# The second query-key product on 64 rows, in a two-group attention block

## The chip, the core and the metric

The kernel runs on one core of one Trainium2 chip. The metric is the time on the device in microseconds (us). A second number is the span of a profiled execution, from its first to its last instruction.

Five engines work side by side: TensorE (PE in the profile, with its weight loads shown apart as PEld), VectorE (DVE), ScalarE (ACT), GpSimd (POOL), and SyncE (SP), which only issues transfers here. A matmul on PE takes a stationary tile, loaded ahead of it by a weight load, and a moving tile; the dimension that is summed over lies on the partitions, of which there are 128. A "row" below is one such partition.

## The reference

One layer of a hybrid encoder block on 1024 tokens of width 1024: one input projection, two kinds of attention of 8 heads each, gates, an output projection, and a layer norm. Cut to what matters:

```python
h = einsum('bsd,de->bse', x, w_in)
q_a, k_a, v_a, z_a, q_b, k_b, v_b, z_b = split(h)
# group A: tokens form a 16 x 64 grid, each query sees a window of 8 x 16
s = einsum('bqhd,biqjhd->bhqij', q_r, k_win) * scale + rel_bias
y_a = softmax(s) @ v_win
# group B: |i - j| <= 128, rotary q and k, 2 key heads for 8 query heads, a sink logit
s = einsum('bnqkgd,bnjkd->bnkgqj', qb, k_band) * scale, masked
y_b = softmax([s, sink])[..., :-1] @ v_band
mixed = concatenate([y_a * silu(z_a), y_b * silu(z_b)])
x = layer_norm(alpha * x + mixed @ w_out)
```

All is float32, and a head has 64 dimensions. To keep that precision on faster products, the kernel splits each operand into a high part in float16 (or a rounded float32) and a low part, the rest after the high part is taken off.

## The kernel before

**Stages.** First comes the value projection, in rounded float32. Then 21 column groups of the input projection (`ORDER`) are computed by `project`, each for two halves of the tokens: 48 products per group, three per chunk of the contraction (high by high, high by low, low by high; L354). Six groups run before the attention stage, and the other fifteen run within it as filler between attention products. The output projection (L889) and the layer norm end the kernel.

**The attention stage** is a loop over 128 units (`unit_list`): 64 of the windowed group "b", then 64 of the neighbourhood group "a". A unit is 128 queries of one head. Step i of the loop (L1023) issues the query-key products of unit i (`stage_qk`), the split and transpose of the probabilities of the unit before it (`stage_tr`), for every fourth step the probability-value products of four earlier units (`stage_pv`, L767), as many projection products as a table allows (`pump_to`), and the exponential of unit i (`stage_exp`).

**The stacked tiles.** Pair p holds two heads, j = 0 and 1, which come out of the projection on partitions 0 to 63 and 64 to 127. For each head the kernel keeps three float16 tiles of 128 partitions. In the code a names the 64 partitions on which the head is made (64j to 64j + 63), and o the other 64.

- `qs` (`split_q`): the high part of q on a, the low part on o.
- `ks` "kh" (`split_k`): the high part of k on a, and a copy of it on o.
- `ks` "kl" (`split_k`): the low part of k on a, and a copy of it on o.

Two products of 128 rows, accumulated in one bank of PSUM, then give (high q + low q) by high k (L704) and (high q + low q) by low k (L705). Both use the same 128 queries of `qs` as the stationary tile; the moving tile is 256, 384 or 288 columns of "kh" or "kl". DVE's fused bias, scale and row minimum (L712) reads the sum.

**Who makes them.** For the neighbourhood group, `split_k` is called with no rotary step (`dep` is None): ACT writes the high part out of PSUM (L233), DVE the low part (L239), and POOL copies each to the other 64 partitions (`dup_`, L271). For the windowed group the source is the rotated k; ACT makes the high part (L235), DVE or POOL the low one (L241), and POOL copies both. The windowed k is made once, in the first six groups, for its two heads and two halves of tokens, and each of its heads serves four heads of q, two with j = 0 and two with j = 1; the neighbourhood k of four pairs, two heads and two halves within the attention stage.

**Order.** The order of instructions on each engine is the order in which the program issues them. Within the loop, small operations wait in a list per engine (`enq`) and `pop` issues a few per step: two on POOL, one or two on DVE and ACT. An operation can be popped once those that it depends on were issued in an earlier step. `need` issues an operation, and what it depends on, at once where a later stage can't go on without it: before the first unit of a head, `need(*stk_ops[...])` (L1047 to L1050) forces out whatever of the stacked tiles isn't issued. A bank for the projection is reused once the operations that read it (`groups`) are issued; for k these are the low-part operations.

Of the kernel before, what the change touches and what calls it, by code (L numbers as in the profile page):

```python
# [53 lines left out]
def hybrid_block(ctx, tc, xT, x, wt, wv, wo, bias, sink, gain, lbias, cos, sin, bmask, out):  # L54
    nc = tc.nc
# [10 lines left out]
    def bank(tag):  # L66
        bufs = {"pj": 2, "s": 4, "t": 2}[tag]
        return (ps1 if bufs == 1 else ps2).tile([128, 512], F32, tag=tag, name=f"ps_{tag}", bufs=bufs)
# [68 lines left out]
    def enq(eng, fn, *deps, prio=1, after=0):  # L137
        op = Op(eng, fn, deps, prio)
        if clock["step"] is not None:
            queues[eng].append(op)  # L140
        elif after:
            events.setdefault(ran[0] + after, []).append(op.emit)
        else:
            op.emit()
        return op
# [10 lines left out]
    def need(*ops):  # L156
        for op in ops:
            if op.step is None:
                need(*op.deps)
                queues[op.eng].remove(op)  # L160
                op.emit()
# [35 lines left out]
    w_ops, stk_ops, load_ops = {}, {}, {}  # L197
# [27 lines left out]
    def own(kind, p, j):  # L225
        if (kind, p, j) not in stks:
            stks[kind, p, j] = stk(kind)
        return stks[kind, p, j]

    def split_hl(h, l, src, scaled, eng):  # L230
        def hi():
            if scaled:
                nc.scalar.activation(h(), src, AF.Copy, scale=QSCALE)  # L233
            else:
                nc.scalar.copy(h(), src)  # L235

        def lo():
            if scaled:
                nc.vector.scalar_tensor_tensor(l(), src, QSCALE, h(), op0=ALU.mult, op1=ALU.subtract)  # L239
            else:  # L240
                (nc.gpsimd if eng == "pool" else nc.vector).tensor_sub(l(), src, h())  # L241

        return hi, lo
# [15 lines left out]
    def split_k(p, half, src, dep=None):  # L259
        sl = slice(512 * half, 512 * half + 512)  # L260
        ops = []
        prio = 0 if dep is None else 1
        eng = "pool" if dep and clock["step"] is not None else "dve"
        for j in range(2):
            a, o = slice(64 * j, 64 * j + 64), slice(64 - 64 * j, 128 - 64 * j)
            hi, lo = split_hl(lambda j=j, a=a: own("kh", p, j)[a, sl], lambda j=j, a=a: own("kl", p, j)[a, sl],
                              src[a], dep is None, eng)

            def dup_(w, j=j, a=a, o=o):
                t = own(w, p, j)  # L270
                nc.gpsimd.tensor_copy(t[o, sl], t[a, sl])  # L271

            o1 = enq("act", hi, dep, prio=prio, after=28 if dep else 0)
            o2 = enq(eng, lo, o1, prio=prio, after=32 if dep else 0)
            ops.append(o2)
            dup = [enq("pool", lambda d=dup_: d("kh"), o1, after=32 if dep else 0),
                   enq("pool", lambda d=dup_: d("kl"), o2, after=36 if dep else 0)]
            stk_ops.setdefault((p, j, half), []).extend(dup)
        return ops

    def rope(ps, half):
# [12 lines left out]
    def evac(name, half, ps):  # L294
        sl = slice(512 * half, 512 * half + 512)
        kind = name.rstrip("0123")
        p = int(name[-1]) if name[-1].isdigit() else 0
        n = ORDER.index(name)
        if kind in ("kb", "qb"):
            raw, o1, o5 = rope(ps, half)  # L300
            if kind == "kb":
                split_k("b", half, raw, o5)
            else:
                split_q(f"b{p}", half, raw, o5)
            return [o1]
        if kind == "k":
            return split_k(p, half, ps)
        if kind == "q":
            return split_q(p, half, ps)
        e = 4 + p if kind == "zb" else p  # L310
        if half == 0:
            zt[e] = zslot(f"z{e}", ZTAG.get(name, "z"))
        if name in ORDER[:3]:
            nc.scalar.activation(zt[e][:, sl], ps, AF.Silu, scale=inv[:, n:n + 1])
            return []
        half_inv = invt[:, 0:1] if n < NPRO else invt[:, 1:2]
        o = enq("act", lambda: nc.scalar.activation(zt[e][:, sl], ps, AF.Tanh, scale=half_inv), prio=0)
        o2 = enq("dve", lambda: nc.vector.scalar_tensor_tensor(
            zt[e][:, sl], zt[e][:, sl], 1.0, ps, op0=ALU.add, op1=ALU.mult), o, prio=0)
        stk_ops.setdefault(name, []).append(o2)  # L320
        return [o2]
# [58 lines left out]
    with ExitStack() as vctx:  # L380
# [5 lines left out]
        ps = bank("t")  # L386
# [139 lines left out]
        for i in range(8):  # L526
# [5 lines left out]
            ps = bank(tags[i])  # L532
# [124 lines left out]
    def geom(u):  # L657
        g, p, j, t, _ = u
        if g == "a":
            b, half = t  # L660
            w = WINW[b]
            return NKEY[b], [4 * w] * 3
        lo, hi = max(t - 1, 0), min(t + 2, 8)
        return 128 * (hi - lo), [128] * (hi - lo)
# [19 lines left out]
    def stage_qk(u):  # L684
        g, p, j, t, _ = u
        n, _c = geom(u)
        ps = bank("s")
        if g == "a":
            b, half = t
            q = stks["q", p, j][:, 512 * half + 128 * b:512 * half + 128 * b + 128]  # L690
            sl = [stks[w, p, j].rearrange("p (r c) -> p r c", c=GW)[
                :, 4 * half:4 * half + 12, WIN0[b]:WIN0[b] + WINW[b]] for w in ("kh", "kl")]
            bias_t, op = st.pop((u, "b"))
            need(op)
            init = 3e38
        else:
            q = stks["q", f"b{p}", j][:, 128 * t:128 * t + 128]
            lo = max(t - 1, 0) * 128
            kv = p // 2
            sl = [stks[w, "b", kv][:, lo:lo + n] for w in ("kh", "kl")]  # L700
            bias_t = bm[:, 128 if t == 0 else 0:(128 if t == 0 else 0) + n]
            h = 2 * p + j
            init = nsk[:, h:h + 1]
        nc.tensor.matmul(ps[:, :n], q, sl[0], start=True, stop=False)  # L704
        nc.tensor.matmul(ps[:, :n], q, sl[1], start=False, stop=True)  # L705
        s0 = sns[units.index(u) % 2]
        sn = s0[:, 384 - n:]
        if g == "b" and t < 2:
            nc.vector.tensor_copy(s0[:, 384:385], nsk[:, h:h + 1])
        nm = ap.tile([128, 1], F32, tag="nm", name="nm", bufs=6)  # L710
        c = min(p, 1) if g == "b" else 2
        nc.vector.tensor_tensor_reduce(sn[:, :n], ps[:, :n], bias_t, sg[:, c:c + 1], init,  # L712
                                       op0=ALU.add, op1=ALU.min, accum_out=nm)
        st[u, "sn"] = sn
        st[u, "ps"] = ps
        st[u, "nm"] = nm
# [28 lines left out]
    def quad(q):  # L745
        g, p, j, t, _ = units[4 * q]
        return g, p, j, t // 4 if g == "b" else t[0] // 2
# [275 lines left out]
    for i in range(-LD, NU + LO):  # L1023
# [21 lines left out]
        if i < NU:  # L1045
            u = units[i]
            if u[3] in (0, 4):  # L1047
                need(*stk_ops[f"b{u[1]}", u[2], u[3] // 4])
            if u[3] == (0, 0):
                need(*stk_ops[u[1], u[2], 0], *stk_ops[u[1], u[2], 1])  # L1050
            stage_qk(u)
        q, m = divmod(i - LP - 3, 4)
# [9 lines left out]
        if m in (0, 2) and 0 <= q < NU // 4:  # L1062
            g, p, j, h = quad(q)
# [88 lines left out]
```

## Time and profile before

| what | value |
|---|---|
| median of three runs | 466.0 us (464.41 to 466.36) |
| the profiled execution | 467.47 us |
| its span | 465.7 us |
| mean granted clock of TensorE | 0.992 |
| matmuls on PE | 3239 |
| L704 and L705, executions each | 128 |
| copies of L271 on POOL | 40, between 107.7 and 332.2 us |
| first and last second product (L705) | 124.7 and 365.8 us |

In a row of grouped instructions stand the line, the engine, the operation, the tiles written and read, the shape and the count; then the busy time, the mean of one in ns, and the idle time of the engine just ahead of them with what ended it. "128*128 128x384" means a stationary tile of 128 rows by 128 columns and a moving tile of 128 rows by 384 columns. PE's records overlap: one starts before the one ahead has ended, so the distance between two starts, and not the length of a record, is what a product takes of the engine's time. A line of the table by stretches gives the stretch, its length, and for each engine the busy time and number of instructions, then the granted clock.

### The profile page before, as it was taken

How to read it: one execution, taken by the hardware profiler on the slowest of the kernel's cores; microseconds unless marked ns; L12 is line 12 of the kernel's file. 1: busy time of each engine (PE TensorE's matmuls, PEld its weight loads, DVE VectorE, ACT ScalarE, POOL GpSimd, SP SyncE). 2: the span in 40 equal slices, each digit the busy share in tenths (PEclk: the TensorE clock that was granted, in tenths of full speed). 3: DMA queues.
4: the chain of work that ended last, by engine and by line, in shares of the span. 5: the costliest groups of instructions: out<-in, count | busy, mean ns of one | idle time of the engine just before them, and what ended most of it. 6: DMA issues, size and time to landing. Idle time of an engine off the chain costs nothing.

```text
span 465.7 us, 9385 instructions
## 1 busy us (share of the span) xinstructions
PE 447.5 (96%) x3239; PEld 294.5 (63%) x3239; DVE 336.8 (72%) x807; ACT 288.3 (62%) x665; POOL 228.4 (49%) x235
## 2 busy tenths in 40 slices
PE   8999999999999899999999999999998789999992
PEld 6999964444455555555655555555465578888882
DVE  4887947439987677787888878877778349099734
ACT  4748569766588767887778777776877424012101
POOL 0004934638668459685246676445835244007621
PEclk9999999999999999999999999999999899999998
DMA  7887287971178999454799899999999995004511
GB/s 232 285 308 277 82 269 252 302 249 29 62 135 223 232 219 156 85 100 101 137 201 199 178 197 204 207 188 207 199 215 194 207 300 209 0 1 145 195 60 52
DMA packets 136463, 82.61 MB, mean 177 GB/s; under 512 B 101344, under 2 KB 117728, under 8 KB 136160
## 3 DMA queue, kind: packets, MB, share of 16 engines
q1 hardware_dynamic: 136272, 81.87, 74.0%
q8 instruction: 25, 0.41, 0.4%
q14 instruction: 22, 0.18, 0.2%
q10 hardware_dynamic: 144, 0.15, 0.1%
HBM read 51.58 MB, written 9.96 MB: 132 GB/s over the span
## 4 chain that ended last, share of the span: by engine, by line
PE 86%; DMA 5%; DVE 4%; issue 2%; ACT 2%; SPq 0%; DVEq 0%; ACTq 0%
PE ps_pj L354 43%; PE ps_s L889 8%; PE ps_t L767 6%; PE ps_s L428 6%; PE ps_pj L889 5%; PE ps_t L889 5%; DMA tr<-split 4%; PE ps_s L704 4%; PE ps_s L705 4%; PE ps_pj L428 3%; PE ps_t L428 3%; PE ps_t L787 1%; DMA xraw<-in_xT 1%; DVE qs L239 1%; ACT split L738 1%
## 5 line engine op out<-in xcount | busy, mean ns | idle before, releaser
L354 PE MATMUL ps_pj<-xf,wh 128*128 128x512 f16 x672 | 202.1, 379 | 0.9 <-DVE qs L239 0.6
L354 PE MATMUL ps_pj<-xf,wl 128*128 128x512 f16 x336 | 127.3, 379 | 0.0
L354 PEld LDWEIGHTS <-wh 128*128 128x128 f16 x672 | 63.5, 98 | 62.1 <-DVE ks L239 1.0
L728 ACT ACTIVATE ps_s<-sn,nm 128x385 f32<-128x385 f32 (+3 forms) x128 | 70.3, 549 | 37.6 <-DVE nm L712 36.7
L739 DVE SCALAR_TENSOR_TENSOR split<-ps_s,split 128x384 f16<-128x384 f32 (+2 forms) x128 | 65.7, 513 | 30.7 <-ACT split L738 29.4
L738 ACT ACTIVATE split<-ps_s 128x384 f16<-128x384 f32 (+2 forms) x128 | 57.5, 449 | 5.6 <-DMA tr<-split 4.0
L354 PEld LDWEIGHTS <-wl 128*128 128x128 f16 x336 | 32.9, 98 | 37.5
L712 DVE CUSTOM_DVE_ANT_0 sn<-ps_s,bm,nsk 128x384 f32<-128x384 f32 (+1 forms) x64 | 40.8, 637 | 7.9 <-PE ps_s L705 7.4
L712 DVE CUSTOM_DVE_ANT_0 sn<-ps_s,bias,sg 128x288 f32<-128x288 f32 (+1 forms) x64 | 36.0, 563 | 13.8 <-PE ps_s L705 6.7
L767 PEld LDWEIGHTS <-tr 128*128 128x128 f16 (+1 forms) x1104 | 37.1, 98 | 10.7 <-DMA tr<-split 7.5
L889 PE MATMUL ps_s<-wo,m 128*128 128x512 f32 (+1 forms) x192 | 43.6, 379 | 0.0
L185 POOL TENSOR_SCALAR wr<-wr,wsc 128x512 f32<-128x512 f32 x26 | 20.6, 792 | 41.8 <-ACT wh L180 33.8
L704 PE MATMUL ps_s<-ks,qs 128*128 128x384 f16 (+2 forms) x128 | 40.0, 312 | 0.0
L705 PE MATMUL ps_s<-ks,qs 128*128 128x384 f16 (+2 forms) x128 | 39.9, 312 | 0.0
L889 PEld LDWEIGHTS ps_s<-wo,m 128*128 128x128 f32 x192 | 34.3, 188 | 6.9
L944 ACT ACTIVATE sd<-mv,eps 128x1 f32<-128x1 f32 x8 | 2.4, 295 | 52.0 <-DVE mv L942 48.0
L186 POOL TENSOR_TENSOR wl<-wr,wh 128x512 f16<-128x512 f32 x26 | 32.6, 1255 | 2.2
L679 POOL TENSOR_SCALAR bias<-bias,rsg 128x576 f32<-128x576 f32 (+1 forms) x24 | 19.2, 798 | 28.1 <-DMA bias<-in_bias 24.2
L271 POOL COPY ks<-ks 64x512 f16<-64x512 f16 x40 | 26.8, 673 | 10.6 <-DVE ks L239 4.3
L981 POOL TENSOR_TENSOR xr<-xr,gb 128x512 f32<-128x512 f32 x7 | 10.3, 1480 | 40.7 <-ACT xr L978 40.7
L889 PE MATMUL ps_pj<-wo,m 128*128 128x512 f32 (+1 forms) x120 | 30.2, 390 | 0.0
L428 PE MATMUL ps_s<-wvh,x 128*128 128x320 f32 x128 | 29.6, 310 | 0.0
(147 smaller groups left out, 831.1 us busy)
## 6 DMA issues: line engine op xcount, KB each, us to landing
xraw<-in_xT SPq DMA_DIRECT2D x31, 256.0 KB, 4.5
ws<-in_wt SPq DMA_DIRECT2D x15, 512.0 KB, 5.4
wr<-in_wt SPq DMA_DIRECT2D x26, 256.0 KB, 3.3
bias<-in_bias SPq DMA_DIRECT2D x16, 288.0 KB, 3.7
wor<-in_wo SPq DMA_DIRECT2D x16, 256.0 KB, 4.2
xr<-in_x SPq DMA_DIRECT2D x8, 512.0 KB, 5.2
out<-xr SPq DMA_DIRECT2D x14, 256.0 KB, 2.2
bias<-in_bias SPq DMA_DIRECT2D x8, 384.0 KB, 4.2
```

What stands on the lines that cost most here:

```text
L186: nc.gpsimd.tensor_sub(l, raw, h)
L271: nc.gpsimd.tensor_copy(t[o, sl], t[a, sl])
L354: nc.tensor.matmul(ps, a[:, k % 4, :], mv, start=(k == 0 and i == 0), stop=(k == KT - 1 and i == 2))
L428: nc.tensor.matmul(ps[:, :320], lh[t // 4, k][:, ts], rh[k][:, cs], start=(k == 0 and i == 0), stop=(k == KT - 1 and i == 2))
L704: nc.tensor.matmul(ps[:, :n], q, sl[0], start=True, stop=False)
L705: nc.tensor.matmul(ps[:, :n], q, sl[1], start=False, stop=True)
L712: nc.vector.tensor_tensor_reduce(sn[:, :n], ps[:, :n], bias_t, sg[:, c:c + 1], init, op0=ALU.add, op1=ALU.min, accum_out=nm)
L728: nc.scalar.activation(pt[:, :m], sn[:, :m], AF.Exp, bias=nm, scale=-1.0, accum_out=sm[:, k:k + 1])
L738: nc.scalar.activation(hl[:, :m, 0, :c], src, AF.Copy, scale=PSCALE)
L739: nc.vector.scalar_tensor_tensor(hl[:, :m, 1, :c], src, PSCALE, hl[:, :m, 0, :c], op0=ALU.mult, op1=ALU.subtract)
L767: nc.tensor.matmul(ps[:, HD * m:HD * m + HD], a, b_, start=(i == 0), stop=(i == len(mms) - 1))
L889: nc.tensor.matmul(ps, lh[:, ts], rh[:, cs], start=(e == EO[0] and i == 0), stop=(e == EO[-1] and i == 2))
```

## The change

The second product takes only the 64 rows a, on which the high part of q and the first copy of the low part of k lie; low q by low k is no longer computed. `stage_qk` slices both operands:

```diff
         nc.tensor.matmul(ps[:, :n], q, sl[0], start=True, stop=False)
-        nc.tensor.matmul(ps[:, :n], q, sl[1], start=False, stop=True)
+        lo = slice(64 * j, 64 * j + 64)
+        nc.tensor.matmul(ps[:, :n], q[lo], sl[1][lo], start=False, stop=True)
```

In `split_k` the copy of the low part is issued only with a rotary step, so for the windowed k; for the neighbourhood k, the operation that a unit needs is then the low part itself:

```diff
-            dup = [enq("pool", lambda d=dup_: d("kh"), o1, after=32 if dep else 0),
-                   enq("pool", lambda d=dup_: d("kl"), o2, after=36 if dep else 0)]
-            stk_ops.setdefault((p, j, half), []).extend(dup)
+            stk_ops.setdefault((p, j, half), []).append(enq("pool", lambda d=dup_: d("kh"), o1, after=32 if dep else 0))
+            if dep:
+                o2 = enq("pool", lambda d=dup_: d("kl"), o2, after=36)
+            stk_ops[p, j, half].append(o2)
```

The windowed k needs its second copy of the low part: a head of q has its high part on the partitions that its own j gives, and the head of k that it uses may have been made on the other 64. In the neighbourhood group q and k of a head share j. The number of products, their columns, and every transfer stay as they were.

## The prediction

> **What bounds the kernel now.** I read the page's first part, then a table of engine time by stage, and then one stretch of the attention stage in order of time. On the first two lines, TensorE (PE) is busy for 96% of the span, well ahead of VectorE (DVE).
>
> ```profile
> span 465.7 us, 9385 instructions
> PE 447.5 (96%) x3239; PEld 294.5 (63%) x3239; DVE 336.8 (72%) x807; ACT 288.3 (62%) x665; POOL 228.4 (49%) x235
> ```
>
> A share over the whole span hides where the engine is full, so the next view cuts the stage in which the changed product runs, 124 to 378 us, into three stretches. The columns are length, busy time of each engine with its instruction count, granted clock, DMA share and rate.
>
> ```profile
> core 0: us, PE busy (x) PEld busy (x) DVE busy (x) ACT busy (x) POOL busy (x), PEclk, DMA share, GB/s
> 124.00:174.00 50.00, 48.46 (x388) 26.75 (x387) 38.10 (x111) 39.33 (x98) 28.98 (x28) 1.00 0.86 191
> 174.00:354.00 180.00, 179.14 (x1635) 103.38 (x1633) 145.47 (x402) 141.40 (x366) 107.88 (x123) 1.00 0.93 171
> 354.00:378.00 24.00, 18.53 (x154) 13.27 (x152) 11.29 (x31) 10.11 (x27) 8.35 (x7) 0.93 1.16 215
> ```
>
> From 174 to 354 us PE is busy for 179.14 of 180 us at a granted clock of 1.00. Nothing added to PE here has idle time to fall into: it lengthens the kernel one for one. GpSimd (POOL) is busy for 107.88 of the same 180 us, and no share of the chain that ended last is its own:
>
> ```profile
> PE 86%; DMA 5%; DVE 4%; issue 2%; ACT 2%; SPq 0%; DVEq 0%; ACTq 0%
> ```
>
> A busy PE can still be slack if its records are padded, so the third view is PE alone, in order of time, at 338 to 347 us. Each line has start, duration, line, tiles, stationary rows*columns, moving shape.
>
> ```profile
> 338.15 0.29 PE L705 MATMUL ps_s<-ks,qs 128*128 128x288 f16 x1
> 338.28 1.22 PE L767 MATMUL ps_t<-va,tr 96*128 96x64 f16 x36
> 339.33 0.38 PE L354 MATMUL ps_pj<-xf,wl 128*128 128x512 f16 x1
> ...
> 340.41 0.33 PE L704 MATMUL ps_s<-ks,qs 128*128 128x384 f16 x1
> 340.57 0.33 PE L705 MATMUL ps_s<-ks,qs 128*128 128x384 f16 x1
> 340.74 0.38 PE L354 MATMUL ps_pj<-xf,wh 128*128 128x512 f16 x1
> 340.95 0.38 PE L354 MATMUL ps_pj<-xf,wl 128*128 128x512 f16 x1
> ...
> 345.60 1.22 PE L767 MATMUL ps_t<-va,tr 128*128 128x64 f16 x36
> 346.65 0.38 PE L354 MATMUL ps_pj<-xf,wl 128*128 128x512 f16 x1
> ```
>
> The second query-key product (L705) starts 0.16 us after the first (L704), and the projection product behind it 0.17 us later, while each record lasts 0.33 us. So each product is let into the array about 0.16 us before the one ahead of it has ended: 0.33 - 0.16 = 0.17 us of every record is a tail under the next product. This overlap is what the change may disturb.
>
> **The change, part by part.** *The second product at 64 rows.* All 128 executions of L705 drop from 128 contraction rows to 64: rows 0 to 63 of the stacked tiles for the first head of a pair, rows 64 to 127 for the second. The moving columns stay 256 to 384, so I look at what fewer rows do to the streaming itself:
>
> ```profile
> L705 PE MATMUL ps_s<-ks,qs 128*128 128x384 f16 x80 | 26.1, 326 | 0.0
> L705 PE MATMUL ps_s<-ks,qs 128*128 128x288 f16 x32 | 9.5, 296 | 0.0
> L705 PE MATMUL ps_s<-ks,qs 128*128 128x256 f16 x16 | 4.4, 273 | 0.0
> L767 PE MATMUL ps_t<-va,tr 96*128 96x64 f16 x288 | 11.6, 193 | 4.8 <-DMA tr<-split 2.8 <-DMA va<-vwin 2.0
> L767 PE MATMUL ps_t<-va,tr 128*128 128x64 f16 x288 | 11.2, 193 | 1.1 <-DMA tr<-split 1.1
> ```
>
> A probability-value product of 96 rows lasts 193 ns, and so does one of 128 rows. Fewer rows save no streaming: 128 x 0 = 0 us.
>
> *The switch from 128 rows to 64 and back.* No row of this trace shows a 64-row product, so I bound it. Lower end: zero. In the stretch above, a block of 36 products of 96 rows between products of 128 rows takes 339.33 - 338.28 = 1.05 us until the next product starts, and a block of 36 with 128 rows 346.65 - 345.60 = 1.05 us, so going to 96 rows and back costs nothing visible. Upper end: the overlap is lost at each switch, so the next product starts only when the one ahead has ended, and its weight load can't be pulled ahead either. The first is 0.17 us. For the second, a run of weight loads has the rate:
>
> ```profile
> 259.55 1.20 PEld L767 LDWEIGHTS <-tr 96*128 96x128 f16 x36
> ...
> L705 PEld LDWEIGHTS <-qs 128*128 128x128 f16 x128 | 12.6, 99 | 14.4
> ```
>
> That is 1.20 / 36 = 0.033 us each, where a record alone reads 0.099 us. So the upper end is 0.17 + 0.03 = 0.20 us a switch. With two switches a unit (into the 64-row product and out of it, since a projection, transpose, probability-value or first query-key product of more rows always follows) there are 2 x 128 = 256. The ends are 0 and 256 x 0.20 = 51 us.
>
> I take the middle, 0.10 us a switch, for this reason. 96 rows starting at partition 0 can be run as the whole array with a quarter left empty. A product whose rows start at partition 64, as for half of the units, enters half-way, and I count on the array being emptied of the 128-row product first. Of the 0.17 us tail, part is the way into the array, which the next product could still overlap, so I take about half of it with a part of the weight load: 256 x 0.10 = 25.6 us. Few of the switches fall into idle time: in the stretch 354 to 378, where PE has 24.00 - 18.53 = 5.5 us idle, the second product runs only six times:
>
> ```profile
> 354.00:378.00 24.00, 2.20 (x6) 0.70 (x6) 0.93 1.16 215
> ```
>
> That hides at most 12 x 0.10 = 1.2 us; I count half, 0.6 us. Sum for the switches: 25 us.
>
> The page "TensorEngine Tiling (Array Packing)" of the Trainium skill, under Key Properties, says that changing the tiling mode drains TensorE, and lists 128, 64 and 32 rows as modes; 96 is not among them, which would explain the free block above. The page "TensorE: Matmul & The Clock Gate" of the Trainium skill, under Phases on the wall clock, gives the drain as about 128 cycles, at 2.4 GHz 53 ns; an estimate by that page alone would be 256 x 0.053 = 13.6 us and a time of about 480 us. No run here shows either yet.
>
> *The copies taken away.* The POOL copies of L271 fall into two groups, those of the windowed k before the attention stage and those of the neighbourhood k within it:
>
> ```profile
> L271 POOL COPY ks<-ks 64x512 f16<-64x512 f16 x40 | 26.8, 673 | 10.6 <-DVE ks L239 4.3 <-ACT ks L233 4.0 <-DVE ks L241 0.6
> ...
> 174.00:354.00 180.00, 19.63 (x32) 1.00 0.93 171
> ```
>
> Half of the 32 are of low parts: 16 x 19.63/32 = 9.8 us of POOL work goes, in a stretch where POOL has 180 - 107.88 = 72 us idle. The eight of the windowed k stay, the low ones among them, since two in four of its q heads take them. What waited for a copy, and every wait of a product that a slow eviction ended in that stretch, are:
>
> ```profile
> DVE sn L712 <- POOL ks L271: 1.4, 2, 0.8
> ...
> PE ps_pj L354 <- DVE qs L239: 0.6, 1, 0.6
> PE ps_pj L354 <- DVE ks L239: 0.3, 1, 0.3
> ```
>
> PE's 0.9 us end on DVE work, not on POOL's, and the 1.4 us on DVE lie beside a full PE. I cost the removal at nothing, with bounds of 0 and a gain of 1.4 + 0.9 = 2.3 us. The cover is PE itself: with PE stretched, evictions and softmax of a unit get later slots and more slack, so no other engine becomes the bound (DVE is next, 145.47 of 180 us).
>
> *The wait that moves.* The second product for the neighbourhood now waits for the low half from DVE (L239) in place of the copy behind it, 0.61 us earlier. POOL's queue closes up by one instruction per removed copy, so the scaling of the bias, the low halves of weights and the rotary steps behind it start earlier or as before. No DMA is added or taken, and SP's queue keeps its order.
>
> *Sum.* The profiled execution took 467.5 us, 1.8 us around its span of 465.7; the three runs have a median of 466.0. 467.5 + 25 - 0 = 492.5 against the profile, and 466.0 + 25 = **491 us** against the median.
>
> **The rivals.** *Full drain*: each switch costs the whole tail and a weight load, 0.20 us. For it speaks that every pair of records overlaps by 0.17 us, so there is that much to lose; against it that part of a record is the way in. It gives 466 + 51 - 1 = 516 us; with the record of 0.099 us for the load in place of 0.033, 256 x 0.27 = 69 us and 534 us at the very end.
>
> *Free rows*: the 64-row product is handled as the 96-row ones are, by leaving rows of the array empty, and the change does not do to the array what I fear. The free 96-row block speaks for it, the start at partition 64 against. Then only POOL's work goes, and the time is 466 us within 1 us.
>
> *Shorter evictions* (the other side): with free rows, the missing copies let the neighbourhood k through earlier at 227 to 247 us and near 336 us, where the two PE waits on evictions stand, and DVE's wait on a copy goes too. The price is the 2.3 us above, so 463.7 us. It decides only if a switch costs under 2.3 / 256 = 0.009 us. For it speaks that POOL loses 9.8 us, against it that no piece of the chain is POOL's.
>
> **How the numbers follow.** About 0.5%, 2.3 us, is what a measurement of this kernel can tell from no change. Partial drain (5 to 40 us, thus 471 to 506) gets 0.49, the full drain 0.20, free rows 0.15, shorter evictions with whatever else the missing copies bring 0.16. Slower is the first two, 0.69; same 0.15; faster 0.16. The likeliest one's own range is 471 to 506 us. The forecast range goes from 463 us, under the evictions' 463.7, to 518 us, over the full drain's 516: what it leaves out is part of the gain case (about 0.07) and the slow weight load (about 0.08).
>
> **What would show it.** With a drain, the start of the 64-row product stands 0.2 to 0.3 us behind L704's and no longer 0.16 us, or the product after L705 starts late by as much; the second product's spacing to it grows, PE's busy share in 174 to 354 us falls, and that stretch grows by about 0.2 us for each unit in it while 62 to 124 us and the output projection behind 378 us keep their lengths. With a full drain the gap nears 0.4 us a unit beyond today's spacing. With free rows the three starts stay 0.16 and 0.17 us apart and the stage keeps its length. POOL should show 24 copies in place of 40. The forecast is wrong if the spacing is unchanged, or if the growth lies in a stretch without the changed product.

## The result, and the profile after

| | before | changed |
|---|---|---|
| median | 465.2 us (463.63 to 466.36, 4 runs) | 487.3 us (486.72 to 489.34, 4 runs) |
| the profiled execution, its span | 467.47, 465.7 us | 489.34, 487.6 us |
| PE busy | 447.5 us | 473.5 us |
| span less PE busy | 18.2 us | 14.1 us |

The changed kernel takes 1.0461 times as long (95% interval 1.0407 to 1.0515): 22 us more. The forecast was 491 us. A fourth run of the kernel before, at 463.63 us, came with the changed kernel's.

The first lines of the changed kernel's page, as above:

```profile
span 487.6 us, 9366 instructions
PE 473.5 (97%) x3239; PEld 284.5 (58%) x3239; DVE 337.1 (69%) x807; ACT 290.3 (60%) x665; POOL 218.3 (45%) x219
```

The same 3239 products keep PE busy for 473.5 - 447.5 = 26.0 us longer. POOL has 16 instructions and 228.4 - 218.3 = 10.1 us less. DVE and ACT do the same work in nearly the same busy time (0.3 and 2.0 us more).

The table by stretches of the changed kernel. The last changed product now starts at 386.3 us instead of 365.8, so the stretches of the later attention stage are cut about 21 us later:

```profile
62.00:124.00 62.00, 62.00 (x295) 28.24 (x293) 40.31 (x87) 45.05 (x81) 37.44 (x38) 1.00 0.62 200
124.00:174.00 50.00, 50.00 (x357) 22.43 (x356) 36.20 (x105) 37.34 (x93) 27.11 (x26) 1.00 0.88 184
174.00:375.00 201.00, 200.85 (x1627) 95.46 (x1623) 147.17 (x403) 143.79 (x368) 99.44 (x109) 1.00 0.81 156
375.00:399.00 24.00, 20.78 (x205) 14.57 (x203) 12.64 (x35) 11.61 (x30) 8.42 (x8) 1.00 1.15 226
399.00:488.00 89.00, 80.12 (x374) 66.31 (x374) 54.17 (x97) 16.88 (x30) 28.61 (x21) 0.95 0.30 108
```

From 124 to 174 us PE gets through 357 products where it got through 388, with the granted clock at 1.00 in both. The stage's idle time shrank: 50.00 - 48.46 = 1.5 us before and none after in this stretch, 0.9 and 0.15 us in the next, 5.5 and 24.00 - 20.78 = 3.2 us in the one where the attention runs out.

Those cuts don't fall on the same work in both kernels. Cut at the first query-key product and behind the last one instead, the kernel before and then the changed one, each with the rest of its span:

```profile
124.60:365.90 241.30, 236.65 (x2086) 136.07 (x2085) 189.99 (x532) 187.39 (x481) 140.52 (x153) 0.99 0.94 179
365.90:465.70 99.80, 88.01 (x469) 72.55 (x467) 59.55 (x108) 20.30 (x38) 32.83 (x24) 0.98 0.40 124
124.43:386.53 262.10, 261.95 (x2086) 124.95 (x2084) 191.07 (x531) 189.09 (x480) 130.44 (x137) 1.00 0.84 165
386.53:487.60 101.07, 89.36 (x468) 73.63 (x467) 58.71 (x109) 20.53 (x40) 32.83 (x24) 0.96 0.40 122
```

The attention stage takes 262.10 - 241.30 = 20.8 us longer: PE is busy for 261.95 - 236.65 = 25.3 us more and idle for 4.65 - 0.15 = 4.5 us less. The output projection and layer norm behind it take 1.3 us longer, at a granted clock of 0.96 instead of 0.98. That part varies from run to run without the change: in the runs described below as no copies, but 128 rows, and as 96 rows, which have the PE time of the kernel before, it takes 101.4 and 102.2 us; in the run with all copies put back, which has the change of rows, 97.7.

Where the time sits is seen only in the starts. PE in order of time, the changed kernel, one unit of 384 columns (lines have moved: L705 is the first query-key product here, L707 the second, and L355 the projection):

```profile
361.52 0.38 PE L355 MATMUL ps_pj<-xf,wh 128*128 128x512 f16 x1
361.74 0.33 PE L705 MATMUL ps_s<-ks,qs 128*128 128x384 f16 x1
362.00 0.33 PE L707 MATMUL ps_s<-ks,qs 64*128 64x384 f16 x1
362.26 0.39 PE L355 MATMUL ps_pj<-xf,wh 128*128 128x512 f16 x1
362.49 0.38 PE L355 MATMUL ps_pj<-xf,wl 128*128 128x512 f16 x1
```

First to second product: 362.00 - 361.74 = 0.26 us, where it was 0.16. Second product to the next: 0.26, where it was 0.17. The records are still 0.33 us long, so they still overlap by 0.07 us: there is no gap to see, and the stall counts as busy time. That is why PE's busy share rose instead of falling. All 80 units of 384 columns show 0.26 to 0.27 us from the first product to the second, whether their 64 rows start at partition 0 or 64. The weight loads of the same unit, the changed kernel first, then the kernel before for its unit at 340.41 us:

```profile
361.52 0.10 PEld L705 LDWEIGHTS <-qs 128*128 128x128 f16 x1
361.99 0.09 PEld L707 LDWEIGHTS <-qs 64*128 64x128 f16 x1 [0.37 <-issue]
362.26 0.10 PEld L355 LDWEIGHTS <-wh 128*128 128x128 f16 x1 [0.17 <-issue]
```

```profile
340.41 0.10 PEld L705 LDWEIGHTS <-qs 128*128 128x128 f16 x1
340.57 0.10 PEld L354 LDWEIGHTS <-wh 128*128 128x128 f16 x1
```

Before, each weight load starts with the product ahead of its own (340.41 for the second product, which starts at 340.57). Around the 64-row product each starts only when its own product does (361.99 and 362.00; 362.26 and 362.26). Neither load is pulled ahead across a change of rows.

### The profile page after: what moved, and what is told of

Read it like the earlier page. It is cut to its first block, busy times and chain, and to the rows that moved or that the text cites. A ratio compares the mean times of both kernels' runs of the same rounds, so it can differ in the third digit from the quotient of the medians.

```text
span 487.6 us, 9366 instructions
## 1 busy us (share of the span) xinstructions
PE 473.5 (97%) x3239; PEld 284.5 (58%) x3239; DVE 337.1 (69%) x807; ACT 290.3 (60%) x665; POOL 218.3 (45%) x219
## 4 chain that ended last, share of the span: by engine, by line
PE 87%; issue 4%; DMA 3%; POOL 3%; DVE 2%; SPq 1%; ACT 1%; POOLq 0%; DVEq 0%; ACTq 0%
PE ps_pj L355 41%; PE ps_s L891 8%; PE ps_t L769 6%; PE ps_s L429 6%; PE ps_s L707 6%; PE ps_pj L891 5%; PE ps_t L891 5%; PE ps_s L705 3%; PE ps_pj L429 3%; PE ps_t L429 3%; DMA tr<-split 2%; PE ps_t L789 2%; POOL wl L186 1%; POOL bias L680 1%; DMA wvraw<-in_wv 1%
## 5 line engine op out<-in xcount | busy, mean ns | idle before, releaser
L355 PE MATMUL ps_pj<-xf,wh 128*128 128x512 f16 x672 | 203.0, 380 | 0.1
L355 PE MATMUL ps_pj<-xf,wl 128*128 128x512 f16 x336 | 127.4, 379 | 0.0
L355 PEld LDWEIGHTS <-wh 128*128 128x128 f16 x672 | 57.8, 98 | 66.4 <-issue 8.7
L741 DVE SCALAR_TENSOR_TENSOR split<-ps_s,split 128x384 f16<-128x384 f32 (+2 forms) x128 | 65.6, 513 | 18.2 <-ACT split L740 17.8
L355 PEld LDWEIGHTS <-wl 128*128 128x128 f16 x336 | 32.9, 98 | 37.7 <-issue 0.7
L891 PE MATMUL ps_s<-wo,m 128*128 128x512 f32 (+1 forms) x192 | 45.0, 389 | 0.0
L707 PE MATMUL ps_s<-ks,qs 64*128 64x384 f16 (+2 forms) x128 | 40.5, 316 | 0.0
L891 PEld LDWEIGHTS ps_s<-wo,m 128*128 128x128 f32 x192 | 35.5, 194 | 7.3
L769 PEld LDWEIGHTS <-tr 128*128 128x128 f16 (+1 forms) x1104 | 35.5, 98 | 7.2 <-DMA tr<-split 4.2
L705 PE MATMUL ps_s<-ks,qs 128*128 128x384 f16 (+2 forms) x128 | 39.7, 310 | 0.0
L707 PEld LDWEIGHTS <-qs 64*128 64x128 f16 x128 | 11.8, 93 | 44.1 <-issue 43.8
L891 PE MATMUL ps_pj<-wo,m 128*128 128x512 f32 (+1 forms) x120 | 28.9, 376 | 0.0
```

The costliest lines, as they stand in the source:

```text
L355: nc.tensor.matmul(ps, a[:, k % 4, :], mv, start=(k == 0 and i == 0), stop=(k == KT - 1 and i == 2))
L707: nc.tensor.matmul(ps[:, :n], q[lo], sl[1][lo], start=False, stop=True)
L741: nc.vector.scalar_tensor_tensor(hl[:, :m, 1, :c], src, PSCALE, hl[:, :m, 0, :c], op0=ALU.mult, op1=ALU.subtract)
L769: nc.tensor.matmul(ps[:, HD * m:HD * m + HD], a, b_, start=(i == 0), stop=(i == len(mms) - 1))
L891: nc.tensor.matmul(ps, lh[:, ts], rh[:, cs], start=(e == EO[0] and i == 0), stop=(e == EO[-1] and i == 2))
```

## The experiments

Two theories stood. By the first, each change between 128 and 64 rows costs about 0.10 us, two a unit, and the copies are worth nothing. By its rivals, each 64-row product costs by itself, or only one that starts at partition 64, or the missing copies play a part.

**The copies put back.** In the changed kernel, every low part is copied again:

```diff
-            if dep:
-                o2 = enq("pool", lambda d=dup_: d("kl"), o2, after=36)
+            o2 = enq("pool", lambda d=dup_: d("kl"), o2, after=36 if dep else 0)
```

> The changed kernel with the 16 copies of the neighbourhood's low parts put back, so the 64-row product alone. If the switches between 128 and 64 rows are the whole loss: 487 us, within 1.5, and the same 0.26 us from the first product to the second. If the missing copies had given back time (evictions that come earlier): 2 us more than the changed kernel, 489 to 490. If the missing copies were part of the loss: under 485.

Measured: 486.6 us (486.42 to 488.88), 1.0435 times the kernel before (1.0363 to 1.0508), the same as the changed kernel. The missing copies gave nothing and cost nothing that these runs could tell.

**No copies, but 128 rows.** The low parts of the neighbourhood lie in four tiles of their own, whose other halves are filled with zeros once. The second product takes 128 rows again, and six `ks` buffers in place of eight and five buffers of split probabilities in place of six make room (not shown). The windowed units keep their copies, so they compute low q by low k again; only the neighbourhood units compute what the changed kernel does:

```diff
-            stks[kind, p, j] = stk(kind)
+            stks[kind, p, j] = klz[j, p % 2] if kind == "kl" and p != "b" else stk(kind)
...
+            klz[j, i] = tiles["kq"].tile([128, S], F16, name=f"klz{j}{i}", bufs=1)
+            nc.gpsimd.memset(klz[j, i][64 - 64 * j:128 - 64 * j, :], 0.0)
```

> The copies of the neighbourhood's low parts left out, and the second product on 128 rows as before: the low parts lie in four tiles whose other 64 rows hold zeros. What is computed is what the changed kernel computes, without a change of rows (one buffer of the split probabilities fewer makes room). If only the change of rows costs: 465 us, within 1. If the missing copies shorten the waits on evictions: 463. If the missing copies or the moved wait cost: up to 487.

Measured: 466.2 us (464.88 to 471.63, 10 runs), 0.9997 times the kernel before (0.9955 to 1.0039). For the neighbourhood units, what the changed kernel saves can be had without its price, but the saving is worth nothing beyond the interval, which leaves room for 2 us. PE's busy time is back, and so are its waits on evictions, which the missing copies were to shorten (the page's first lines, then two of PE's waits, of this run):

```profile
span 464.6 us, 9369 instructions
PE 447.5 (96%) x3239; PEld 294.9 (63%) x3239; DVE 335.1 (72%) x807; ACT 288.1 (62%) x665; POOL 222.2 (48%) x222
```

```profile
PE ps_pj L355 <- DVE qs L239: 0.6, 1, 0.6
...
PE ps_pj L355 <- DVE klz L239: 0.2, 1, 0.2
```

They stand at 0.6 and 0.2 us against 0.6 and 0.3 before. These waits end on DVE's own low parts, so a copy behind them on POOL was never in their way.

**Half as many changes of rows.** Two units' products are issued together, first both of 128 rows, then both of 64:

```diff
-            stage_qk(u)
+            if i % 2 == 0:
+                qk = [stage_qk(units[i]), stage_qk(units[i + 1])]
+                for g in qk * 2:
+                    next(g)
+            list(qk[i % 2])
```

(`stage_qk` yields after each of its two products.)

> The changed kernel, but two units' products are issued together every second step: 128, 128, 64, 64 rows. As many 64-row products, half as many changes of rows. If the cost is by change of rows, 128 changes less at 0.10 us: 475 us, 473 to 477, with the second 64-row product 0.16 us behind the first. If each 64-row product costs by itself, by a weight load that isn't pulled ahead: 487.

Measured: 476.1 us (475.51 to 476.67), 1.0201 times the kernel before (1.0120 to 1.0282). As many 64-row products, about half the loss: by this run's page PE is busy for 460.1 us, 12.6 more than before, where the changed kernel has 26.0 more. A pair of 288 columns in order of time on PE, of this run:

```profile
342.40 0.41 PE L705 MATMUL ps_s<-ks,qs 128*128 128x288 f16 x2
342.74 0.42 PE L708 MATMUL ps_s<-ks,qs 64*128 64x288 f16 x2
343.09 0.39 PE L355 MATMUL ps_pj<-xf,wh 128*128 128x512 f16 x1
```

Two products take 0.34 and two take 0.35 us, start to start. Before, one of 288 columns took 338.28 - 338.15 = 0.13 us, so two take 0.26, and 0.08 and 0.09 us are left for the two changes of rows, which a pair of units now shares. Both products of a pair lie on the same 64 partitions; a change from one half to the other was not tested.

**Twice the 64-row products.** Each second product is cut into two 64-row products of half the columns:

```diff
-        nc.tensor.matmul(ps[:, :n], q[lo], sl[1][lo], start=False, stop=True)
+        m = n // 2
+        for c in (0, 1):
+            kl = sl[1][lo, 6 * c:6 * c + 6] if g == "a" else sl[1][lo, m * c:m * c + m]
+            nc.tensor.matmul(ps[:, m * c:m * c + m], q[lo], kl, start=False, stop=c == 1)
```

> The changed kernel with each second product cut into two 64-row products of half the columns, one behind the other: twice the 64-row products and weight loads, the same changes of rows. If the cost is by change of rows: 487 to 489 us. If each 64-row product costs 0.1 us by itself: 128 x 0.1 = 13 us more, 500.

Measured: 487.6 us (486.59 to 489.17), 1.0449 times the kernel before (1.0377 to 1.0521), the same as the changed kernel. In order of time on PE, of this run:

```profile
344.24 0.33 PE L705 MATMUL ps_s<-ks,qs 128*128 128x384 f16 x1
344.50 0.34 PE L710 MATMUL ps_s<-ks,qs 64*128 64x192 f16 x2
344.77 0.60 PE L355 MATMUL ps_pj<-xf,wh 128*128 128x512 f16 x2
```

Their weight loads, of this run:

```profile
344.50 0.11 PEld L710 LDWEIGHTS <-qs 64*128 64x128 f16 x2 [0.37 <-issue]
```

The two halves take 0.27 us, what one whole product takes in the changed kernel (0.26). Both weight loads are through 0.11 us after the first of them starts. A second 64-row product and its weight load behind a first are free within 0.01 us. With the paired run this settles it: the change of rows costs, not the 64-row product.

**Which rows.** Four runs start from the kernel before, with all its copies, and cut the second product for the heads of one j alone; the others keep 128 rows. The edit is one line, here for the first:

```diff
-        nc.tensor.matmul(ps[:, :n], q, sl[1], start=False, stop=True)
+        lo = slice(0, 64) if j == 0 else slice(0, 128)
+        nc.tensor.matmul(ps[:, :n], q[lo], sl[1][lo], start=False, stop=True)
```

> The kernel before, all copies made, with the second product of each pair's first head on partitions 0 to 63, the second head on 128 rows (windowed heads whose low k lies on either half are served by the copies). If 64 rows cost by the number of rows, wherever they start: 466 + 11 = 477 us. If only a start at partition 64 costs, as the prediction's reason has it: 466.

> The kernel before, all copies made, with the second product of each pair's second head on partitions 64 to 127, the first head on 128 rows. By the number of rows: 477 us. If only a start at partition 64 costs: the whole loss, 487.

With `slice(0, 96) if j == 0`:

> The kernel before, all copies made, with the second product of each pair's first head on partitions 0 to 95: 64 rows of high q and 32 of low q (32 dimensions of low q by low k are left out), the second head on 128 rows. If rows that stay within the four quarters of one array cost nothing, as in the block of probability products: 466 us, within 1. If every change of the number of rows costs 0.10 us: 64 x 2 x 0.10 = 13 us more, 477 to 478.

With `slice(0, 32) if j == 0`:

> As the run with 64 rows on partitions 0 to 63, but on partitions 0 to 31 only: half of the 64 dimensions of high q by low k are left out for the first heads. If a change of rows empties the array whatever the height: 477 us. If the cost grows with the rows that fall away: more, 481 at one and a half times; if it goes with the height that is left: less, 472.

| second product | median | above the kernel before | ratio on record (interval) |
|---|---|---|---|
| 64 rows from partition 0, j = 0 | 477.4 us | 10.6 us | 1.0199 (1.0099 to 1.0298) |
| 64 rows from partition 64, j = 1 | 476.6 us | 9.8 us | 1.0180 (1.0097 to 1.0263) |
| 96 rows from partition 0, j = 0 | 467.0 us | 0.3 us | 1.0014 (0.9969 to 1.0058) |
| 32 rows from partition 0, j = 0 | 476.1 us | 9.3 us | 1.0164 (1.0083 to 1.0246) |

The kernel before was at 466.7 us (463.37 to 468.80, 8 runs) beside these (those of 12 runs that are within 1.5% of its fastest), and the third column goes by it. The ratios for 64 and 32 rows count four more runs of it, at 470.69 to 474.42 us, and come out lower for that. Half of the units give about half of the loss wherever their 64 rows start, 32 rows cost what 64 cost, and 96 rows cost nothing beyond the interval. The starts on PE say the same, first with 96 rows, then with 32 (in order of time, one unit of each run):

```profile
126.16 0.33 PE L704 MATMUL ps_s<-ks,qs 128*128 128x384 f16 x1
126.32 0.33 PE L706 MATMUL ps_s<-ks,qs 96*128 96x384 f16 x1
126.49 0.60 PE L354 MATMUL ps_pj<-xf,wh 128*128 128x512 f16 x2
```

```profile
126.24 0.33 PE L704 MATMUL ps_s<-ks,qs 128*128 128x384 f16 x1
126.50 0.33 PE L706 MATMUL ps_s<-ks,qs 32*128 32x384 f16 x1
126.77 0.60 PE L354 MATMUL ps_pj<-xf,wh 128*128 128x512 f16 x2
```

0.16 and 0.17 us with 96 rows, as with 128; 0.26 and 0.27 with 32, as with 64.

## Why the prediction was right, point by point

**PE has no idle time to hide it: right for the middle of the stage, not for its ends.** Every changed product cost its price in PE time: 25.3 us more busy time in the attention stage. From 174 us on, PE was busy for 179.14 of 180.00 us before and for 200.85 of 201.00 after. But the stage grew by 20.8 us only, because PE's waits shrank, most of all ahead of that stretch and behind it, as worked out below.

**0.10 us a switch, 25.6 us in all: right, and in part by luck.** 25.3 / 256 = 0.10 us, and the starts show it on both sides of the 64-row product. The paired run confirms the count that it goes with. But 0.10 us was the middle between 0 and 0.20, from a trace without any 64-row product, and the reason given for it did not hold.

**The reason for taking the middle: wrong in part.** The prediction took the drain to be due to rows that start at partition 64. By that reason only the units with j = 1, half of them, should pay, and yet the sum counted all 256 switches. 64 rows from partition 0 cost the same 0.10 us a switch, so the count was right and the reason was not. The number of rows decides: 96 belong with 128, 64 and 32 do not. The free 96-row block that it quoted was therefore no evidence for the free rival, and the run with 96 rows in this very place shows that it is not the place either. The Trainium skill, page "TensorEngine Tiling (Array Packing)", Key Properties, says that a change of the tiling mode drains TensorE, with 128, 64 and 32 rows as the modes; these runs agree in that going from 128 rows to 64 or to 32 costs 0.10 us and going to 96 costs nothing.

**How much of it falls into idle time: mis-sized.** The prediction counted 0.6 us, from the six second products in the stretch where PE waits. In the attention stage idle time fell by 4.5 us: 1.5 us of early waits between 124 and 174 us went, 0.7 us of waits on evictions, and 5.5 - 3.2 = 2.3 us of the waits at the stage's end. Elsewhere it grew by 0.4 us, so span less busy time fell by 18.2 - 14.1 = 4.1 us. PE's longest waits, the kernel before and then the changed one, are those for the transposes of the split probabilities:

```profile
PE ps_t L767 <- DMA tr<-split: 5.4, 7, 1.3
PE ps_t L767 <- DMA va<-vwin: 2.0, 1, 2.0
...
PE ps_t L769 <- DMA tr<-split: 3.4, 3, 1.5
```

The changed kernel's list has no wait on va and none on the low parts that DVE makes. A slower PE leaves more time to the transposes, loads and evictions that it waits for, so idle time can shrink far beyond the few products that stand in it. Not all of the 4.5 us need be that: the runs with zeros and with 96 rows, whose PE is as fast as before, have 2.9 and 2.1 us of idle time in this stage, where the one profiled execution of the kernel before has 4.65. 25.6 - 0.6 = 25.0 us was forecast, 26.0 - 4.1 = 21.9 us is what the span shows. Of the 3.7 us by which 491 us lies over 487.3, this term makes 3.5. The rest is small and of both signs: the busy time came out 0.4 us over the forecast, and the kernel before has a median of 465.2 us by four runs where the forecast started from 466.0. That the copies did not bring this is seen in the run with all copies put back: its span less busy time is 484.8 - 472.6 = 12.2 us, by its page:

```profile
span 484.8 us, 9385 instructions
PE 472.6 (97%) x3239; PEld 283.3 (58%) x3239; DVE 336.2 (69%) x807; ACT 290.2 (60%) x665; POOL 228.0 (47%) x235
```

**The copies at nothing: right.** Both ways of testing it, with 64 rows and with 128, moved nothing beyond the intervals. One piece came out otherwise: DVE's wait on copies (L271), whose 1.4 us were to go at best, is 4.6 us in the changed kernel and 7.4 us with all copies put back. Beside a full PE it costs nothing that shows.

**The rivals.** The full drain, 0.20 us a switch and 516 us, is out: it asked for 51 us more on PE and 26.0 came. Free rows are out. Shorter evictions needed a switch under 0.009 us, and the run with zeros shows no gain beyond its interval even without any switch. The estimate by the page "TensorE: Matmul & The Clock Gate" of the Trainium skill, under Phases on the wall clock, 0.053 us a switch and 480 us, counts about half of what the starts show.

**What would show it: one sign was misjudged.** The starts, the unchanged lengths ahead of the stage and POOL's 24 copies came as said. PE's busy share in the stage was to fall and rose, from 179.14 of 180.00 us to 200.85 of 201.00, because the stall lies inside records that overlap. The stage was to grow by about 0.2 us a unit: PE's busy time in it did (25.3 / 128 = 0.20), its length by 20.8 / 128 = 0.16. The part behind the stage was to keep its length and took 1.3 us longer, which the lower clock there goes with.

Whether the 0.10 us is the emptying of the array, the weight load that is no longer pulled ahead, or some of each was not separated. An estimate from the traces gives no more than bounds: by the rate of a run of weight loads, 0.033 us each, a load that is wholly exposed would leave about 0.07 us for the rest; by the 0.09 us that the record of a 64-row load lasts, it would leave almost nothing.

## What to carry to other kernels

A product on 64 rows is not cheaper than one on 128, and on a full TensorE it cost 0.10 us here to go to it and 0.10 us to come back. Fill the other half with zeros or a copy on an engine that has time, stop at 96 rows (tested from partition 0), or issue the 64-row products next to each other, so that several share one pair of changes. Read the distance between starts on PE: the busy share and the record lengths hide such a stall.

## What the runs showed of the hardware that was not expected

The price of a change of rows does not depend on which half of the partitions is used, on whether 64 or 32 rows are used, or, within 0.01 us, on the columns of the first product: with 288 columns the second product starts 0.21 to 0.22 us behind the first, with 384 columns 0.26, each about 0.10 us more than with 128 rows. The starts on PE for 288 columns, in the changed kernel:

```profile
353.48 0.29 PE L705 MATMUL ps_s<-ks,qs 128*128 128x288 f16 x1
353.69 0.29 PE L707 MATMUL ps_s<-ks,qs 64*128 64x288 f16 x1
353.92 0.39 PE L355 MATMUL ps_pj<-xf,wh 128*128 128x512 f16 x1
```
